# One TensorE product per head and step in the RWKV-7 scan: two kinds of scores and the token-major keys from the same weights

## The chip, the cores and the metric

The kernel runs on one core of a Trainium2 chip. A core has five engines that work through their own instruction streams in order: TensorE (PE; its weight loads are listed apart as PEld), VectorE (DVE), ScalarE (ACT), GpSimd (POOL) and SyncE (SP). SP, ACT and POOL also issue transfers, which 16 DMA engines carry out. The metric is the device time of one execution in microseconds (us); where several executions are compared, their medians are.

## The reference, cut to what matters

The program is a trunk of two layers on 1024 latent tokens and 256 context tokens of width 1024, all in 32-bit floats. The change lies in layer 1, the bidirectional RWKV-7 time mixing. It has 16 heads of width 64. For each head and each of two directions a 64x64 state runs over the context and then over the latent tokens:

```python
def step(S, inp):
    w_t, k_t, v_t, kk_t, kka_t = inp[:5]
    S = (S * w_t[:, :, None, :]
         - jnp.einsum('bhij,bhj->bhi', S, kk_t)[..., None] * kka_t[:, :, None, :]
         + v_t[..., None] * k_t[:, :, None, :])
    y = jnp.einsum('bhij,bhj->bhi', S, inp[5]) if emit else None
    return S, y
```

Here `kk` is the normalised key that is removed, `kka` is that key times a gate, `k` the key that is written, `v` the value, `r` the receptance that reads the state out. Only latent tokens are read out (`emit`).

## The kernel before, in words

The scan is done in chunks of 64 tokens. There are 20 chunks in each direction: steps 0 to 3 are the context, 4 to 19 the latent tokens. Inside a chunk the recurrence becomes matrix products over the 64 tokens; between chunks only the state `SS` is carried. 16 heads are kept as 8 pairs: the first head of a pair (e = 0) in partitions 0 to 63, the second (e = 1) in 64 to 127.

For each step s and direction d an earlier stage has written four feature arrays, which `load` (L1566) brings to one of four buffers `FT` of 128 partitions x 8 pairs x 4 arrays x 64 tokens. The arrays are: 0, the receptance r with its decay; 1, the removed key with its decay; 2 and 3, the two scaled keys (kka and k, divided by the decay). Context chunks have no array 0.

From these, one step early (for n = s + 1), three things are made:

- `scores_k` (L1596): for each head the 64x64 product of array 3 with array 1, into the PSUM tile `sa`. DVE multiplies it with a mask and puts it into partitions 64 to 127 of `Z`. `stack` (L1591) has ACT copy array 1 into partitions 0 to 63 of `Z`.
- `scores_r` (L1608), latent steps only: arrays 2 and 3 together as weights (128 columns) times array 0, into two PSUM tiles `sr`; DVE masks them into `Q`.
- `token_major` (L1626): PE transposes arrays 2 and 3 (4 pairs at a time, tile `tm`), ACT copies them to `TM`, so that the tokens lie along the partitions.

These PSUM tiles turn in a ring of four banks (`scps`). Then come the parts that hang on the state, each with 16 products (each counted twice in the trace, as every 32-bit product is two passes), in another ring of four banks (`chps`):

- `chain_x` (L1664): `Z` times `D`, where `D` holds the carried state in its lower half and the values in its upper half; ACT copies it to `XS`.
- `chain_u` (L1672): the inverse of a triangular matrix (`TT`) times `XS`; ACT writes the negated result into `D` (L1679).
- `readout_state` (L1681) and `readout_values` (L1693), latent steps only: array 0 times the state, and `Q` times `D`, into one tile `yp`; ACT copies it, SP stores it.
- `chain_s` (L1709): `TM` times `D`; DVE adds the old state (L1722) and scales by the decay (L1726).
- `carry` (L1731): in the following iteration, ACT copies the new state into the next `D` (L1736).

`compose1` and `compose2` put the triangular inverses together from blocks of 32 (products of 32x32, tile `p`), once per step, in the iteration of direction 1. `background` supplies work for DVE that `fill` strews between the parts: inversions of the blocks (`scan_invert`, L1511 and L1515) until about step 13, then readout work of the first tokens. `fill` takes on average 1.5, then 2.45, later 1 items.

The loop over steps and directions is under a manual schedule: every engine's instructions stand in the order in which the code emits them. For one iteration (s, d) it is:

```python
load_values(n, d); chain_x(s, d); carry()
scores_k(n, d); token_major(n, d, 0); fill()
chain_u(s, d); [compose1(n)]; token_major(n, d, 4); stack(n, d); fill()
readout_state(s, d); chain_s(s, d); readout_values(s, d); fill()
scores_r(n, d); [compose2(n)]; load(s + 2, d); fill()
```

The two in brackets are there for d = 1 only. After the loop, `readout_weight` reuses the buffers of `Z`, `Q` and `TM` for split weights.

Of the kernel before, what the change touches and what calls it, by code (L numbers as in the profile page):

```python
# [19 lines left out]
D = 1024  # L20
# [19 lines left out]
CH = 64  # L40
# [18 lines left out]
class Trunk:  # L59
# [1466 lines left out]
    def l1_scan(self):  # L1526
        nc, a = self.nc, self.a
        with ExitStack() as es:
# [5 lines left out]
            scps = self.pool(es, "scps1", 4, PSUM)  # L1534
# [3 lines left out]
            FTs = [cp.tile([128, 8, 4, CH], F32, name=f"FT{i}") for i in range(4)]  # L1538
# [4 lines left out]
            st = (slice(0, 64), slice(64, 128))  # L1543

# [9 lines left out]
            W = {s: dict(lat=s >= NCC, F=[0, 0], Z=[0, 0], Q=[0, 0], TM=[0, 0], D=[0, 0], Y=[0, 0]) for s in range(NSTEP)}  # L1554
# [6 lines left out]
            def load(s, d):  # L1561

                w = W[s]
                F = w["F"][d] = FTs[(2 * s + d) % 4]
                f0 = 0 if w["lat"] else 1
                (nc.scalar if s == 0 else nc.gpsimd).dma_start(out=F[:, :, f0:], in_=self.ft[s, d, :, :, f0:])  # L1566
# [24 lines left out]
            def stack(s, d):  # L1591

                for e in range(2):
                    nc.scalar.copy(out=W[s]["Z"][d][0:64, :, e], in_=W[s]["F"][d][st[e], :, 1])

            def scores_k(s, d):  # L1596
                F = W[s]["F"][d]
                Z = W[s]["Z"][d] = zp.tile([128, 8, 2, CH], F32, tag="Z", name="Z")
                sa = scps.tile([128, 8, CH], F32, tag="sc", name="sa")
                for h in range(8):  # L1600
                    for e in range(2):
                        nc.tensor.matmul(out=sa[st[e], h], lhsT=F[st[e], h, 3], rhs=F[st[e], h, 1], start=True, stop=True)  # L1602
                for e in range(2):
                    nc.vector.tensor_tensor(
                        out=Z[64:128, :, e], in0=sa[st[e]], in1=masks[st[e], d, 2:3].to_broadcast([64, 8, CH]), op=ALU.mult
                    )

            def scores_r(s, d):  # L1608

                w = W[s]  # L1610
                if not w["lat"]:
                    return
                F = w["F"][d]
                Q = w["Q"][d] = zp.tile([128, 8, 2, CH], F32, tag="Q", name="Q")
                sr = [scps.tile([128, 8, CH], F32, tag="sc", name="sr") for _ in range(2)]
                for h in range(8):
                    for e in range(2):
                        nc.tensor.matmul(  # L1618
                            out=sr[e][:, h], lhsT=F[st[e], h, 2:4].rearrange("p a t -> p (a t)"), rhs=F[st[e], h, 0], start=True, stop=True
# [598 lines left out]
```

## Time and profile before

| | |
|---|---|
| time before, median of 3 runs | 3549.33 us (3537.39 to 3551.44) |
| profiled execution, its own time | 3559.48 us |
| its span, first to last instruction | 3557.6 us |
| PE busy | 3327.8 us (94%), 26794 instructions |
| PE weight load busy | 2790.3 us (78%) |
| DVE busy | 2054.7 us (58%) |
| ACT busy | 1432.3 us (40%) |
| POOL busy | 342.3 us (10%) |
| mean granted TensorE clock | 0.962 |

The scan's first state product starts at 2212.8 us and its last step ends near 2682 us. Busy shares of the whole span are means over very different stages, so the table is no guide to the scan; stages have to be looked at one by one. A line such as "L1604 DVE TENSOR_TENSOR Z<-sa,masks 64x512" reads: line of the kernel, engine, operation, written tile, read tiles, shape of the output. "Idle before" is the time for which the engine stood idle just ahead of these instructions, with what ended it. "issue" is time in which an engine waited for nothing that the profile shows.

### The profile page before, as it was taken

What the parts mean: (1) busy time and instruction counts of PE and PEld (TensorE: products, weight loads), DVE (VectorE), ACT (ScalarE), POOL (GpSimd) and SP (SyncE); (2) the same over time, 40 slices, a digit from 0 to 9 for tenths busy, and PEclk for the clock granted to TensorE, in tenths of its full rate; (3) what the DMA queues carried; (4) which work ended last, traced back from release to release, by engine and by line L of the source; (5) the groups of instructions that cost most, each with busy time, mean ns of one, the idle gap of its engine ahead of it and who ended that gap; (6) DMA issues with size and microseconds to landing.
All of it is one profiled execution on the core that took longest, in us unless ns stands there. A gap on an engine that the chain in (4) does not pass through costs nothing. (4 is left out here: it accounts for less than half of the span.)

```text
span 3557.6 us, 64666 instructions
## 1 busy us (share of the span) xinstructions
PE 3327.8 (94%) x26794; PEld 2790.3 (78%) x26794; DVE 2054.7 (58%) x3879; ACT 1432.3 (40%) x2667; POOL 342.3 (10%) x450
## 2 busy tenths in 40 slices
PE   8999889999999999989988876899988899999998
PEld 4787767888888888868878776788886788888887
DVE  4255555344444444596658996888775734444446
ACT  4244446312121211266767664655554521111112
POOL 0010110000000000024420001010031200000000
PEclk9999989999999999999989897899988999999999
DMA  8433344222222211143227678777773411111112
GB/s 274 151 92 87 97 131 130 89 83 83 83 84 83 74 46 36 42 148 99 71 69 221 210 233 241 170 185 201 200 204 104 164 50 48 48 48 48 48 48 77
DMA packets 426517, 409.24 MB, mean 115 GB/s; under 512 B 149664, under 2 KB 360480, under 8 KB 422128
## 3 DMA queue, kind: packets, MB, share of 16 engines
q1 hardware_dynamic: 405376, 321.55, 30.8%
q0 software_dynamic: 18624, 81.80, 6.8%
q8 instruction: 210, 3.44, 0.4%
q10 hardware_dynamic: 2224, 1.77, 0.2%
q14 instruction: 83, 0.68, 0.1%
HBM read 292.54 MB, written 112.49 MB: 114 GB/s over the span
## 5 line engine op out<-in xcount | busy, mean ns | idle before, releaser
L916 DVE TENSOR_TENSOR yacc<-yps,yacc 128x512 f32<-128x512 f32 x540 | 369.7, 690 | 305.2 <-PE yps L93 304.8
L74 ACT CAST wh<-st 128x1024 fp32r<-128x1024 f32 x160 | 165.0, 1049 | 759.8 <-PE yps L93 557.8
L93 PE MATMUL yps<-wh,xh 128*128 128x512 f32 x1152 | 453.8, 394 | 5.0 <-DVE yacc L916 3.4
L93 PE MATMUL yps<-wh,xl 128*128 128x512 f32 x1152 | 449.0, 390 | 0.7 <-DVE xl L75 0.7
L93 PE MATMUL yps<-wl,xh 128*128 128x512 f32 x1152 | 449.4, 390 | 0.0
L75 DVE TENSOR_TENSOR wl<-st,wh 128x1024 fp32r<-128x1024 f32 x160 | 194.2, 1228 | 277.4 <-ACT wh L74 277.2
L93 PE MATMUL acc<-h2h,wh 128*128 128x426 f32 (+3 forms) x768 | 275.1, 358 | 3.0 <-ACT y L671 3.0
L93 PEld LDWEIGHTS yps<-wh,xh 128*128 128x128 f32 x1152 | 216.4, 188 | 73.0 <-DVE yacc L916 14.0
L93 PE MATMUL acc<-h2h,wl 128*128 128x426 f32 (+3 forms) x768 | 273.6, 356 | 0.0
L93 PE MATMUL acc<-h2l,wh 128*128 128x426 f32 (+3 forms) x768 | 273.4, 356 | 0.0
L93 PEld LDWEIGHTS yps<-wh,xl 128*128 128x128 f32 x1152 | 216.5, 188 | 47.9 <-DVE xl L75 2.3
L93 PEld LDWEIGHTS yps<-wl,xh 128*128 128x128 f32 x1152 | 216.7, 188 | 44.9 <-issue 1.7
L898 DVE TENSOR_TENSOR r<-r 128x428 f32<-128x428 f32 (+4 forms) x164 | 102.4, 624 | 241.9 <-ACT r L897 241.9
L93 PE MATMUL acc<-mh,wh 128*128 128x256 f32 (+1 forms) x640 | 214.8, 337 | 4.3 <-ACT mh L74 4.2
L93 PE MATMUL acc<-ml,wh 128*128 128x256 f32 (+1 forms) x640 | 214.0, 334 | 0.0
L93 PE MATMUL acc<-mh,wl 128*128 128x256 f32 (+1 forms) x640 | 213.4, 334 | 0.0
L93 PE MATMUL acc<-h2bh,wh 128*128 128x512 f32 (+3 forms) x544 | 211.3, 388 | 1.4 <-ACT wh L74 0.7
L93 PE MATMUL acc<-h2bl,wh 128*128 128x512 f32 (+3 forms) x544 | 211.1, 388 | 1.0 <-DVE h2bl L288 1.0
L93 PE MATMUL acc<-h2bh,wl 128*128 128x512 f32 (+3 forms) x544 | 210.9, 388 | 0.3 <-DVE wl L75 0.3
L897 ACT ACTIVATE r<-acc 128x428 f32<-128x428 f32 (+4 forms) x164 | 89.1, 543 | 293.0 <-PE acc L93 267.9
L93 PEld LDWEIGHTS acc<-h2h,wh 128*128 128x128 f32 x768 | 144.6, 188 | 15.9 <-issue 5.1
L74 ACT CAST xh<-r 128x428 fp32r<-128x428 f32 (+4 forms) x164 | 93.2, 569 | 148.1 <-DVE r L898 148.1
(319 smaller groups left out, 7042.1 us busy)
## 6 DMA issues: line engine op xcount, KB each, us to landing
st<-in_mlp_w SPq DMA_DIRECT2D x128, 512.0 KB
ft<-F SPq DMA_DIRECT2D x64, 512.0 KB
FT<-ft POOLq DMA_DIRECT2D x32, 1024.0 KB, 7.1
adas<-in_ada_w POOLq DMA_DIRECT2D x112, 256.0 KB, 3.8
adas<-in_ada_w SPq DMA_DIRECT2D x80, 256.0 KB
x<-x SPq DMA_DIRECT2D x28, 512.0 KB
bias<-in_bias SPq DMA_DIRECT2D x64, 192.0 KB
ls<-ls SPq DMA_DIRECT2D x80, 128.0 KB
```

The costliest lines, as they stand in the source:

```text
L74: self.nc.scalar.copy(out=hi, in_=src)
L75: self.nc.vector.tensor_tensor(out=lo, in0=src, in1=hi.bitcast(F32), op=ALU.subtract)
L93: self.nc.tensor.matmul(out=ps, lhsT=lhs[x], rhs=rhs[y], start=first and i == 0, stop=last and i == 2)
L897: nc.scalar.activation(out=r, in_=ps, func=AF.Relu)
L898: nc.vector.tensor_tensor(out=r, in0=r, in1=r, op=ALU.mult)
L916: nc.vector.tensor_tensor(out=yacc[t][:, n], in0=ps, in1=yacc[t][:, n], op=ALU.add)
```

## The change

- The buffers `FT` get a fifth slot in front, filled once with the identity by eight DVE copies. The arrays move up by one: 1 is r, 2 the removed key, 3 and 4 the scaled keys. `load` writes slots 1 (or 2) to 4.
- `scores_k`, `scores_r` and `token_major` become one function `scores(s, d, g)` for two pairs, g from 0 to 3. For each head one product has slots 3 and 4 as weights (128 columns) and slots 0, 1, 2 as moving data (192 columns): identity, r and removed key. So it gives the transposed scaled keys, the scores of r and the scores of the removed key. In context steps the r slot is left out, in the last step the identity (128 columns each).
- The result of a group goes into a tile of two PSUM banks, one for each e; there are two such tiles in place of four of one bank.
- `Z` and `Q` become one tile `ZQ`. DVE masks both kinds of scores of a group with one operation; for r's half this is as before, for the other half it also writes partitions 0 to 63, which `stack` then overwrites with the removed key. ACT copies a group's transposed keys to `TM`: four copies in place of two.
- `stack` moves from its place behind `token_major(n, d, 4)` to the end of `carry`, in the following iteration.
- `p1` is written over the block `G` in place of a tile of its own, the state's sum into `SS` itself in place of `t`; the readout's weights 3, 4, 6 and 7 each take one `ZQ` buffer.

```diff
-            scps = self.pool(es, "scps1", 4, PSUM)
+            scps = self.pool(es, "scps1", 2, PSUM)
...
-            FTs = [cp.tile([128, 8, 4, CH], F32, name=f"FT{i}") for i in range(4)]
+            FTs = [cp.tile([128, 8, 5, CH], F32, name=f"FT{i}") for i in range(4)]
...
+            for t in FTs:
+                for e in range(2):
+                    nc.vector.tensor_copy(out=t[st[e], :, 0], in_=self.ident[st[e], st[e]].unsqueeze(1).to_broadcast([64, 8, CH]))
...
-                (nc.scalar if s == 0 else nc.gpsimd).dma_start(out=F[:, :, f0:], in_=self.ft[s, d, :, :, f0:])
+                (nc.scalar if s == 0 else nc.gpsimd).dma_start(out=F[:, :, 1 + f0:], in_=self.ft[s, d, :, :, f0:])
...
-                    nc.scalar.copy(out=W[s]["Z"][d][0:64, :, e], in_=W[s]["F"][d][st[e], :, 1])
...
+                    nc.scalar.copy(out=W[s]["ZQ"][d][0:64, :, e, 1], in_=W[s]["F"][d][st[e], :, 2])
+
+            def scores(s, d, g):
+
+
                 w = W[s]
...
                 F = w["F"][d]
...
+                more = s + 1 < NSTEP
+                if g == 0:
+                    w["ZQ"][d] = zp.tile([128, 8, 2, 2, CH], F32, tag="ZQ", name="ZQ")
+                    if more:
+                        w["TM"][d] = zp.tile([128, 8, 128], F32, tag="TM", name="TM")
+                ps = scps.tile([128, 2, 512], F32, tag="sc", name="sc")
+                p4 = ps[:, :, 0:384].rearrange("p e (j f t) -> p j e f t", j=2, f=3)
+                f = slice(0, 3) if w["lat"] and more else slice(1, 3) if w["lat"] else slice(0, 3, 2)
+                for j in range(2):
                     for e in range(2):
                         nc.tensor.matmul(
...
+                            out=p4[:, j, e, f], lhsT=F[st[e], 2 * g + j, 3:5].rearrange("p a t -> p (a t)"), rhs=F[st[e], 2 * g + j, f],
+                            start=True, stop=True,
                         )
...
+                hs = slice(2 * g, 2 * g + 2)
+                if w["lat"]:
                     nc.vector.tensor_tensor(
...
+                        out=w["ZQ"][d][:, hs].rearrange("p j e f t -> p j e (f t)"),
+                        in0=ps[:, :, 0:384].rearrange("p e (j n) -> p j e n", j=2)[:, :, :, CH:],
+                        in1=masks[:, d, 1:3].rearrange("p f t -> p (f t)").unsqueeze(1).unsqueeze(1).to_broadcast([128, 2, 2, 2 * CH]),
+                        op=ALU.mult,
                     )
...
+                else:
+                    nc.vector.tensor_tensor(
+                        out=w["ZQ"][d][64:128, hs, :, 1], in0=p4[64:128, :, :, 2],
+                        in1=masks[64:128, d, 2:3].unsqueeze(1).to_broadcast([64, 2, 2, CH]), op=ALU.mult,
                     )
...
+                if more:
+                    nc.scalar.copy(out=w["TM"][d][:, hs].rearrange("p j (e i) -> p j e i", e=2), in_=p4[:, :, :, 0])
...
-                w["p1"] = zs.tile([128, 2, 8, 32], F32, tag="p1s", name="p1s", bufs=1)
+                w["p1"] = w["G"]
...
+                    nc.vector.tensor_tensor(out=SS[d], in0=sp, in1=SS[d], op=ALU.add)
+                    src = SS[d]
...
+                    stack(s, d)
...
-                    scores_k(n, d)
-                    if n + 1 < NSTEP:
-                        token_major(n, d, 0)
+                    for g in range(2):
+                        scores(n, d, g)
                     fill()
                     chain_u(s, d)
                     if d:
                         compose1(n)
-                    if n + 1 < NSTEP:
-                        token_major(n, d, 4)
-                    stack(n, d)
+                    scores(n, d, 2)
                     fill()
                     readout_state(s, d)
                     chain_s(s, d)
                     readout_values(s, d)
                     fill()
-                    scores_r(n, d)
+                    scores(n, d, 3)
                     if d:
                         compose2(n)
```

More of the change, by code (lines that the diff above doesn't have):

```diff
@@ L1552, in rows_of @@
                 return t[c * CH:(c + 1) * CH]
-            W = {s: dict(lat=s >= NCC, F=[0, 0], Z=[0, 0], Q=[0, 0], TM=[0, 0], D=[0, 0], Y=[0, 0]) for s in range(NSTEP)}
+            W = {s: dict(lat=s >= NCC, F=[0, 0], ZQ=[0, 0], TM=[0, 0], D=[0, 0], Y=[0, 0]) for s in range(NSTEP)}
             lt_, ltt_ = self.lt_, self.ltt_
@@ L1593, in stack @@
                 for e in range(2):
[L1594 to L1606, printed above, removed]
@@ L1668, in chain_x @@
                     for e in range(2):
-                        nc.tensor.matmul(out=xp[st[e], h], lhsT=w["Z"][d][:, h, e], rhs=w["D"][d][:, h, e], start=True, stop=True)
+                        nc.tensor.matmul(out=xp[st[e], h], lhsT=w["ZQ"][d][:, h, e, 1], rhs=w["D"][d][:, h, e], start=True, stop=True)
                 nc.scalar.copy(out=XSs[d], in_=xp)
@@ L1688, in readout_state @@
                         nc.tensor.matmul(
-                            out=yp[st[e], h], lhsT=w["F"][d][st[e], h, 0], rhs=SS[d][st[e], h], start=h == 0, stop=True,
+                            out=yp[st[e], h], lhsT=w["F"][d][st[e], h, 1], rhs=SS[d][st[e], h], start=h == 0, stop=True,
                             skip_group_check=True,
@@ L1700, in readout_values @@
                         nc.tensor.matmul(
-                            out=yp[st[e], h], lhsT=w["Q"][d][:, h, e], rhs=w["D"][d][:, h, e], start=False, stop=True, skip_group_check=True
+                            out=yp[st[e], h], lhsT=w["ZQ"][d][:, h, e, 0], rhs=w["D"][d][:, h, e], start=False, stop=True, skip_group_check=True
                         )
@@ L1781, in l1_scan @@
             for d in range(2):
-                scores_k(0, d)
+                for g in range(4):
+                    scores(0, d, g)
                 stack(0, d)
-                for h0 in (0, 4):
-                    token_major(0, d, h0)
                 load(1, d)
@@ L1886, in readout_weight @@
         ip, zp = self.rwp
-        pool, tag = {
-            8: (ip, "M"), 0: (ip, "X"), 1: (zp, "TM"), 2: (ip, "BK"), 3: (zp, "Z"), 4: (zp, "Q"), 5: (zp, "TM"), 6: (zp, "Z"), 7: (zp, "Q"),
-        }[k]
-        w = [pool.tile([128, D], F32R, tag=tag, name=f"rwo{i}{k}") for i in "hl"]
+        if k in (3, 4, 6, 7):
+            w = zp.tile([128, 2, D], F32R, tag="ZQ", name=f"rwo{k}")
+            w = [w[:, i] for i in range(2)]
+        else:
+            pool, tag = {8: (ip, "M"), 0: (ip, "X"), 1: (zp, "TM"), 2: (ip, "BK"), 5: (zp, "TM")}[k]
+            w = [pool.tile([128, D], F32R, tag=tag, name=f"rwo{i}{k}") for i in "hl"]
         self.split(w[0], w[1], self.rst.pop(k))
```

21 lines of the change are left out of this document (removed).

## The prediction

> **What bounds the kernel now.** The change touches only the scan, so I read the table of stages first. Columns: stretch, length, then busy time of PE, PE weight load, DVE, ACT, POOL (instructions in brackets), granted clock, DMA share, GB/s.
>
> ```profile
> span 3557.6 us, 64666 instructions
> ```
>
> ```profile
> 2212.80:2288.70 75.90, 64.97 (x1668) 57.78 (x1666) 57.42 (x136) 50.44 (x86) 7.61 (x12) 0.91 0.81 174
> 2288.70:2538.20 249.50, 228.81 (x5926) 209.98 (x5922) 216.65 (x521) 141.57 (x240) 23.67 (x41) 0.93 0.68 183
> 2538.20:2667.80 129.60, 114.88 (x2947) 105.59 (x2944) 84.06 (x100) 77.31 (x129) 35.75 (x23) 0.92 0.76 218
> ```
>
> These are steps 0 to 3 (mainly context), 4 to 13 (block inversions run between the steps on DVE) and 14 to 18 (early readout runs between them). PE looks like the bound of all three. The chain of waits in order of time (start, length, work) shows one iteration of one direction, 2394.20 to 2403.64, and what follows the other:
>
> ```profile
> 2388.28 1.90 PE sp L1716 x32
> ...
> 2394.20 1.08 PE xp L1669 x32
> 2395.29 1.08 PE sa L1602 x32
> 2396.36 0.59 PE tm L1632 x4
> 2396.95 1.08 PE up L1677 x32
> 2398.03 0.59 PE tm L1632 x4
> 2398.61 1.08 PE yp L1688 x32
> 2399.69 1.08 PE sp L1716 x32
> 2400.78 0.93 PE yp L1700 x32
> 2401.71 1.93 PE sr L1618 x32
> ...
> 2414.48 1.13 PE p L1658 x64
> 2415.61 1.08 PE xp L1669 x32
> 2416.69 1.08 PE sa L1602 x32
> ```
>
> PE has no gap there: 9.44 us for direction 0 and 11.97 (to 2415.61) for direction 1, which also builds the inverses. But the second view, DVE's groups in steps 4 to 13 (busy, mean | idle before them), says that DVE is no less full:
>
> ```profile
> L1515 DVE TENSOR_TENSOR X<-X,tmp 128x112 f32<-128x112 f32 (+15 forms) x196 | 66.8, 341 | 6.7
> L1511 DVE TENSOR_TENSOR tmp<-X,M 128x112 f32<-128x112 f32 (+15 forms) x196 | 66.4, 339 | 5.1
> L1604 DVE TENSOR_TENSOR Z<-sa,masks 64x512 f32<-64x512 f32 x40 | 27.6, 690 | 9.7 <-PE sa L1602 8.9
> L1622 DVE TENSOR_TENSOR Q<-sr,masks 128x512 f32<-128x512 f32 x40 | 25.6, 682 | 0.1
> L1722 DVE TENSOR_TENSOR t<-sp,SS 128x512 f32<-128x512 f32 x21 | 14.5, 692 | 8.9 <-PE sp L1716 8.4
> ```
>
> Of DVE's idle 249.50 - 216.65 = 32.9 us only 8.9 + 8.4 = 17.3 are waits for PE. The other 15.6 are gaps of some 0.03 us between instructions (6.7 us over 196 in the first row). If DVE never waited, the stage would take 249.5 - 17.3 = 232.2 us, 11.6 per iteration: more than the 10.7 that PE needs on average for 9.44 and 11.97. DVE and PE are bounds together, and PE's stalls are what keeps DVE waiting.
>
> **The change, part by part: PE.** An iteration loses sa, two tm and sr: 1.08 + 0.59 + 0.59 + 1.93 = 4.19 us. It gains 16 products of 64 rows by 128 weight columns with 192 moving columns. Two heads of a pair sit in different row halves and run together, and each product is two passes, so that is 16 pair-passes. Layer 0 has the same form with 256 and 384 columns:
>
> ```profile
> 314.12 0.70 PE L731 MATMUL sc<-kT,qT 64*128 64x256 f32 x4
> 314.66 0.81 PE L736 MATMUL sl<-kT,qT 64*128 64x384 f32 x4
> ```
>
> ```profile
> L736 PE MATMUL sl<-kT,qT x128: 482/482/844, 160.8 to 459.4; 64*128 64x384 f32 x128
> ```
>
> Four sl records last 0.81 us in all and the last one 0.482, so the second pair-pass starts 0.33 us after the first with 384 columns; sr gives 1.93/16 = 0.12 with 64 columns. If streaming covers the weight load, 192 columns cost half of sl's: 0.16, or 2.6 us for 16. If load and stream add up, the line through 0.12 and 0.33 gives 0.20, or 3.2 us. The sc row decides: from 314.12 to 314.66 lie one load and two pair-passes of 256 columns. The line's 0.245 for each would leave 0.05 us for the load; the proportion's 0.22 leaves 0.10, close to sr's 0.12, which with so few columns is nearly all load. I take 2.6, a saving of 1.6 us (other end 1.0). Context steps use 128 columns: between 0.12 and 0.16 per pair-pass, some 1.9 us against 1.08 + 1.18; the last step 1.9 against 1.08 + 1.93. PE's work shrinks by 30 x 1.6 + 2 x 1.1 + 8 x 0.35 = 53 us at most, the whole prize.
>
> The Trainium skill, "TensorE: Matmul & The Clock Gate", Part 3, on what overlaps, speaks against it: a weight load overlaps a running product only in another row group, and here each pair fills both. By that rule the 3.2 us or more would hold. It is counted below as a mechanism.
>
> **DVE.** Two key masks (2 x 0.690) and two score masks (2 x 0.682) become four operations of 128x512 from PSUM, 4 x 0.69: 2.76 for 2.74, nothing saved. The operand shapes are new; 2.6 to 3.2 bounds them. The addition that now writes in place costs the same. So the 232.2 us stand, and steps 4 to 13 can gain from 0 to 17.3 us. With 1.6 us more slack per iteration PE catches up part of a stall (20.7 us idle in the stage, and a granted clock of 0.93). Against it stand two score buffers (of two banks each) instead of four, which tie PE to DVE's last two mask operations. I take half: -9.
>
> **ACT.** Its queue in the same iteration, and the nearest row for the smaller copy:
>
> ```profile
> 2395.44 0.58 ACT L1670 COPY XS<-xp 128x512 f32<-128x512 f32 x1
> 2396.05 1.26 ACT L1736 COPY D<-SS 64x512 f32<-64x512 f32 x2
> 2397.21 0.57 ACT L1635 COPY TM<-tm 128x512 f32<-128x512 f32 x1
> 2398.14 1.21 ACT L1679 ACTIVATE D<-up 64x512 f32<-64x512 f32 x2 [0.35 <-PE up L1677]
> 2399.37 0.58 ACT L1635 COPY TM<-tm 128x512 f32<-128x512 f32 x1
> 2399.98 1.25 ACT L1594 COPY Z<-FT 64x512 f32<-64x512 f32 x2
> ```
>
> ```profile
> L1251 ACT COPY vt<-acc 128x256 f32<-128x256 f32 x40 | 15.2, 380 | 1.3 <-PE acc L93 1.0 <-issue 0.4
> ```
>
> Two copies of 128x512 (1.15) become four of 128x256 (4 x 0.38 = 1.52). The two key copies (1.25) move from behind the negated copy (L1679) to right behind the carried states, and there they wait for DVE's fourth mask. In front of the negated copy then stand XS 0.58, D 1.26, keys 1.25 and two copies of 0.76, so it starts 3.85 us after xp's end (2.85 above: 2398.14 against 2395.29) and ends at 5.1. What is queued behind it: the second sp, and readout values. From xp's end PE has two groups of products (1.3 us), up (1.08), then the third group, which needs the first group's copy: 0.58 + 1.26 + 1.25 + 0.38 = 3.5. PE stands idle from 2.4 to 3.5 in direction 0; in direction 1 the 1.13 us of inverse products fill it. Third group 0.65, yp 1.08: sp is reached at 5.2, just past the copy's 5.1. So ACT takes back 1.1 of the 1.6 us in direction 0 and nothing in direction 1: 1.05 saved on average.
>
> In steps 14 to 18 DVE has room (84.06 of 129.60) and this sum applies: 10 iterations x 1.05 = 10.5 us, but readout work also stands in DVE's and ACT's queues ahead of masks and copies. I take -5 (bounds -16, all of PE's 1.6, and +3).
>
> In steps 0 to 2 there is no readout product to cover the negated copy; PE already waits for it:
>
> ```profile
> 2239.18 1.09 PE L1716 MATMUL sp<-D,TM 128*64 128x64 f32 x29 [0.29 <-ACT D L1679]
> ```
>
> Six iterations with the copy 1.25 + 0.76 - 0.57 = 1.44 later are +8.6 us at most, 0 at least where a stall is longer; +4.
>
> **DMA, and the start.** The buffer has five slots, so a load lands in runs of 1 KB instead of one of 8 KB per partition. The context loads (runs of 768 bytes) are the nearest rows:
>
> ```profile
> FT<-ft POOLq DMA_DIRECT2D x32, 1024.0 KB, 7.1
> ...
> FT<-ft POOLq DMA_DIRECT2D x6, 768.0 KB, 9.3
> ```
>
> ```profile
> 2400.23 0.53 POOL L1566 DMA_DIRECT2D FT<-ft  x1 [9.70 <-ACT TM L1635]
> ```
>
> By bytes the context rate would give 12.4 us, so 7.1 to 12.4. The load issued at 2400.23 is first read at 2416.69, 16.5 us later: hidden, with 4 us to spare at the worse end. The Trainium skill, "DMA: Bandwidth & Descriptors", Specifications, puts full rate at 512 bytes and more, which would leave 7.1. If the cover were gone, the 5 us would fall on each of 32 iterations.
>
> Eight copies of the identity (64x512, at most 8 x 0.69 = 5.5 us) come onto DVE at the scan's start, among the last feature units. An idle stretch there nearly holds them:
>
> ```profile
> 2191.88 0.42 DVE L1388 TENSOR_TENSOR ks<-kd 128x256 f32<-128x256 f32 x1 [5.12 <-PE bp L1413]
> ```
>
> I count +1.5 (0 to +8, should the larger buffers or the copies delay the first loads). Fewer tiles (p1s, t), the merged buffers and the readout weights in them cost nothing: their old readers are done an iteration earlier.
>
> **Sum.** -9 - 5 + 4 + 1.5 = -8.5 us. The profiled execution took 3559.48 us (span and 1.9 around it), 10 above the median; the difference is carried over: 3549.33 - 8.5 = 3541. Own range 3527 to 3553.
>
> **Rivals.** *PE's gain arrives whole.* DVE's 17.3 us of waiting vanish and steps 14 to 18 save 10 x 1.6: -33, or 3516. For it: DVE's waits are all for PE. Against: ACT's order in direction 0.
>
> *ACT becomes the bound* (the other side). The key copies wait behind DVE's fourth mask and stand in front of the negated copy. It decides as soon as that mask ends over 1.8 us (0.58 + 1.26) past xp's end and DVE is not the slower anyway. In 16 iterations (0 to 2, 14 to 18) then +1.44 each and no PE gain: +23, or 3572. For it: readout operations between the masks. Against: ACT is busy 77.31 of 129.60 us.
>
> *The products are dearer.* Load and stream add up, 3.2 us for 4.19; ACT's 1.1 leaves nothing, steps 0 to 3 and the start keep +5.5: 3555. The sl and sc rows speak against it. The same result if loads come late now and then.
>
> The clock acts in all cases: sp took 1.90 us at 2388.28 and 1.08 at 2399.69. More idle PE may lower it; where DVE is the bound this costs nothing.
>
> **Chances.** Forecast 0.52, whole gain 0.20, ACT bound 0.13, dearer products 0.15. A measurement here can tell some 0.5%, 17.7 us: below 3531.6 is faster, above 3567.1 slower. Faster: 0.13 of the forecast and 0.19 of the whole gain, 0.32. Slower: 0.11 of ACT and 0.02 of dearer products, 0.13. Same: 0.55. The range reaches from the whole gain to half of ACT's loss: 3514 to 3562.
>
> **What would show it.** Right: the new products take 2.5 to 2.7 us per iteration; PE's busy time in the scan falls by some 45 us while DVE's stays near 217 in steps 4 to 13 and its waits for PE fall below 10; PE waits in front of the third group for ACT or DVE. Wrong: PE idle no longer than before (whole gain), sp waiting for the negated copy in steps 4 to 18 (ACT), pair-passes of 0.2 us, waits on FT loads, or a first xp over 5 us later.

## The result and the profile after

The changed kernel takes 3561.55 us (median of 11 runs, 3557.53 to 3578.39), the kernel before 3547.84 us (11 runs, 3537.39 to 3554.24). The ratio is 1.0051, 95% interval 1.0034 to 1.0067: slower by some half a per cent (13.7 us between the two medians), where a small gain of 8.5 us was forecast. A second set of runs gave 3567.11 us and 1.0047 (1.0034 to 1.0061).

The first profiled execution of the kernel before lay 10 us above its median. The comparison of stages below therefore uses a second one, whose own time was 3548.8 us. The view is the table of stages again (stretch, length, busy time of PE, weight load, DVE, ACT, POOL, granted clock, DMA share, GB/s), for steps 0 to 3, 4 to 13 and 14 to 18. First the kernel before, second execution:

```profile
2210.60:2285.90 75.30, 66.63 (x1668) 59.26 (x1666) 57.53 (x136) 50.43 (x86) 7.60 (x12) 0.88 0.75 176
2285.90:2534.50 248.60, 223.87 (x5924) 205.47 (x5920) 216.15 (x520) 141.35 (x240) 23.69 (x41) 0.96 0.68 184
2534.50:2659.80 125.30, 114.84 (x2950) 105.83 (x2944) 82.80 (x100) 77.20 (x129) 35.33 (x23) 0.92 0.76 223
```

Then the changed kernel, whose profiled execution took 3557.53 us:

```profile
2206.60:2297.00 90.40, 71.88 (x1537) 62.64 (x1536) 64.64 (x163) 49.97 (x99) 9.48 (x12) 0.85 0.73 160
2297.00:2541.10 244.10, 205.32 (x5126) 177.98 (x5120) 204.99 (x507) 141.66 (x280) 30.75 (x42) 0.97 0.71 181
2541.10:2668.90 127.80, 102.90 (x2567) 90.55 (x2560) 81.53 (x99) 77.88 (x146) 38.19 (x23) 0.95 0.78 219
```

PE's busy time falls, from 405.3 to 380.1 us over the three rows. The stages don't follow: 15.1 us are lost in steps 0 to 3, 4.5 won in steps 4 to 13, 2.5 lost in 14 to 18. The scan also begins 4.0 us earlier, which is within the scatter of its start (between 2204 and 2213 us over all the profiles of this case). That makes 9 of the 13.7 us; the other 5 lie between this execution, the fastest of the 11, and the median, and no profile here shows them.

Where PE stands still is plain in the groups of the changed kernel (busy, mean ns | idle before them). The first row is of steps 0 to 3, the second of steps 4 to 13:

```profile
L1614 PE MATMUL sc<-FT 64*128 64x128 f32 (+1 forms) x256 | 28.9, 355 | 14.6 <-ACT TM L1632 11.7 <-issue 3.0
...
L1614 PE MATMUL sc<-FT 64*128 64x192 f32 x640 | 73.0, 351 | 25.6 <-ACT TM L1632 25.5
```

PE stands idle in front of the new products for 14.6 us in steps 0 to 3 (11.7 of them wait for ACT) and 25.6 in steps 4 to 13. Of the 15.1 us that steps 0 to 3 lose, 9.8 are more idle time of PE (18.5 us against 8.7); the other 5.3 are its own busy time (71.88 against 66.63), at a granted clock of 0.85 against 0.88. What ends the wait is ACT's copy of an earlier group to `TM`, which frees a PSUM tile. And that copy waits too. The waits of steps 4 to 13 in the changed kernel (total us, times, longest):

```profile
ACT TM L1632 <- DVE ZQ L1620: 58.3, 30, 4.1
...
PE sc L1614 <- ACT TM L1632: 25.5, 31, 1.7
DVE ZQ L1620 <- PE sc L1614: 17.8, 16, 2.9
...
DVE SS L1718 <- PE sp L1713: 10.1, 9, 1.9
```

ACT's copy waits for DVE's mask of the same PSUM tile, though the copy reads other columns than the mask and nothing that the mask writes. No step of the prediction has a copy wait for the mask of its own tile. DVE's waits for PE, 17.3 us before, are now 27.9.

ACT's queue in an iteration of direction 0 shows at which copy it stands (timeline, idle before in brackets):

```profile
2393.03 0.37 ACT L1632 COPY TM<-sc 128x256 f32<-128x256 f32 x1 [3.01 <-DVE ZQ L1620]
...
2394.49 0.59 ACT L1667 COPY XS<-xp 128x512 f32<-128x512 f32 x1
2395.10 1.26 ACT L1732 COPY D<-SS 64x512 f32<-64x512 f32 x2
2396.38 1.25 ACT L1597 COPY ZQ<-FT 64x512 f32<-64x512 f32 x2
2397.53 0.63 ACT L1632 COPY TM<-sc 128x256 f32<-128x256 f32 x2
2398.06 1.21 ACT L1676 ACTIVATE D<-up 64x512 f32<-64x512 f32 x2
2399.64 0.37 ACT L1632 COPY TM<-sc 128x256 f32<-128x256 f32 x1 [0.37 <-DVE ZQ L1620]
...
2405.80 0.37 ACT L1632 COPY TM<-sc 128x256 f32<-128x256 f32 x1 [3.20 <-DVE ZQ L1620]
2406.07 0.59 ACT L1667 COPY XS<-xp 128x512 f32<-128x512 f32 x1
```

Groups 0 and 1 are copied at 2397.53, group 2 at 2399.64, group 3 at 2405.80. Added up over these rows of all 20 iterations, ACT stands 51.3 us ahead of the copy of group 3, 5.3 ahead of that of group 2 and 0.3 ahead of the other two. The chain of waits says why (start, length, work):

```profile
2397.63 0.28 ACT TM L1632
...
2397.95 0.94 PE sc L1614 x8
...
2401.22 0.69 DVE SS L1718
...
2401.94 0.69 DVE SS L1722
2402.64 0.34 DVE tmp L1511
...
2404.76 0.40 DVE X L1515
2405.16 0.61 DVE ZQ L1620
...
2405.80 0.37 ACT TM L1632
2406.17 0.49 ACT XS L1667
```

Group 3's products were done at 2402.8, but in DVE's queue a fill (three pairs of inversion operations, 2402.64 to 2405.16) stood ahead of its mask. So the mask was late, ACT's copy waited for it, and `XS`, the two carried states and the two key copies stood behind that copy. `xp` was ready at 2403.9; `XS` was copied at 2406.1. The first two rows are the same link at the head of the iteration: group 2's products start as group 0's copy ends.

### The profile page after: what moved, and what is told of

Read it like the earlier page. It is cut to its first block, busy times and chain, and to the rows that moved or that the text cites. A ratio compares the mean times of both kernels' runs of the same rounds, so it can differ in the third digit from the quotient of the medians.

```text
span 3555.8 us, 62116 instructions
## 1 busy us (share of the span) xinstructions
PE 3298.3 (93%) x25466; PEld 2747.9 (77%) x25466; DVE 2050.4 (58%) x3903; ACT 1435.6 (40%) x2743; POOL 353.7 (10%) x450
## 5 line engine op out<-in xcount | busy, mean ns | idle before, releaser
L93 PEld LDWEIGHTS yps<-wh,xh 128*128 128x128 f32 x1152 | 216.2, 188 | 70.7 <-DVE yacc L916 11.7
L1614 PE MATMUL sc<-FT 64*128 64x192 f32 (+1 forms) x1280 | 146.0, 356 | 64.0 <-ACT TM L1632 50.7
L1614 PEld LDWEIGHTS sc<-FT 64*128 64x128 f32 x1280 | 106.1, 205 | 80.3 <-ACT TM L1632 60.8
```

Source lines behind the costliest of these rows:

```text
L93: self.nc.tensor.matmul(out=ps, lhsT=lhs[x], rhs=rhs[y], start=first and i == 0, stop=last and i == 2)
L1614: nc.tensor.matmul(out=p4[:, j, e, f], lhsT=F[st[e], 2 * g + j, 3:5].rearrange("p a t -> p (a t)"), rhs=F[st[e], 2 * g + j, f], start=True ...
```

## The experiments

All times are medians; ratios are against the kernel before, run beside it on the same chip (its medians lay between 3543.9 and 3547.1 us). Stages are lengths in us of steps 0 to 3, 4 to 13 and 14 to 18 in the profiled execution; the last column is how long ACT stood ahead of the copies of groups 0, 1, 2, 3 in steps 4 to 13, added up over ACT's timeline.

| kernel | median | ratio (95%) | 0-3 | 4-13 | 14-18 | ACT ahead of copies 0, 1, 2, 3 |
|---|---|---|---|---|---|---|
| before_again | 3548.80 (one run) | | 75.3 | 248.6 | 125.3 | |
| after_again | 3567.11 | 1.0047 (1.0034 to 1.0061) | 89.2 | 240.7 | 132.3 | 0.0, 0.3, 4.2, 52.0 |
| stack_late | 3553.88 | 1.0019 (1.0010 to 1.0028) | 84.0 | 248.2 | 129.3 | 4.8, 3.2, 1.5, 53.5 |
| stack_before | 3549.85 | 1.0011 (1.0000 to 1.0021) | 81.8 | 241.4 | 124.1 | |
| copy_first | 3564.56 | 1.0040 (1.0027 to 1.0054) | 83.1 | 247.4 | 131.6 | |
| loop_cut | 3576.76 | 1.0077 (1.0064 to 1.0091) | 89.6 | 254.8 | 129.0 | |
| noinv_before | 3547.10 | 1.0008 (0.9993 to 1.0023) | 76.2 | 245.2 | 122.2 | |
| noinv_after | 3542.50 | 0.9998 (0.9983 to 1.0013) | 79.3 | 238.4 | 127.3 | |
| respaced | 3543.80 | 0.9994 (0.9982 to 1.0006) | 81.0 | 244.8 | 118.8 | 4.9, 3.3, 1.7, 49.0 |
| one_fill | 3548.69 | 1.0015 (0.9998 to 1.0031) | 86.3 | 238.3 | 127.4 | 9.1, 3.5, 9.1, 27.7 |
| fills_only | 3544.04 | 0.9989 (0.9975 to 1.0004) | 84.4 | 234.6 | 121.1 | 9.2, 2.9, 36.2, 20.3 |
| late_copy | 3557.01 | 1.0037 (1.0023 to 1.0051) | 89.0 | 243.9 | 133.0 | 1.1, 1.4, 7.8, 9.3 |
| two_runs | 3560.16 | 1.0043 (1.0027 to 1.0059) | 87.0 | 243.4 | 133.5 | 50.2, 5.8, 1.3, 2.4 |
| two_runs_f | 3534.95 | 0.9965 (0.9954 to 0.9977) | 86.2 | 231.2 | 120.4 | 35.5, 5.4, 18.2, 4.6 |
| two_runs_c | 3557.94 | 1.0030 (1.0019 to 1.0040) | 87.7 | 236.0 | 129.7 | |
| two_runs_3f | 3543.23 | 0.9985 (0.9972 to 0.9997) | 77.8 | 241.9 | 128.6 | 13.4, 5.2, 51.2, 5.7 |
| two_runs_stack | 3537.08 | 0.9972 (0.9960 to 0.9984) | 81.4 | 235.0 | 126.8 | 15.0, 3.3, 40.5, 5.3 |
| two_runs_ctx | 3533.11 | 0.9962 (0.9948 to 0.9977) | 81.4 | 232.4 | 122.8 | 37.2, 5.6, 18.9, 3.9 |

A stage of one profiled execution can stand some us off another of the same kernel (244.1 and 240.7, 127.8 and 132.3 for the changed kernel), so single stages are read only where they differ by more, or where two pairs agree.

**The two kernels again,** unaltered:

> The kernel before once more, for a second profile: the first profiled execution was slower than any of its other times, and four profiles of changed kernels have their first scan product at 2205 to 2213 us where that profile has it at 2213. Expected by all theories: the same stage table for the scan within 5 us a stage (steps 0 to 3: 76, 4 to 13: 250, 14 to 18: 130), and a first scan product between 2205 and 2213 us.

> The changed kernel once more, unaltered, for a second profile and a second set of times. Theory 'loop': in every iteration one loop sets the pace: DVE's mask of the last group, the copies of ACT behind it (keys to TM, XS, carried state, removed keys, keys to TM), the third group's products on PE, DVE's mask, fill and state update, and back to the last mask. It expects the ratio to before again near 1.005, ACT's wait for DVE's mask in front of the TM copies again near 58 us in steps 4 to 13, and steps 0 to 3 again 10 to 15 us longer than before. Rival 'chance': the profile pair shows the changed kernel 2 us shorter while the medians show it 14 us longer, so the difference could sit in stalls of the load queues that fall by chance; it expects a ratio between 0.998 and 1.002 and a stage table in which another stage carries the difference.

Measured: 3548.8 and 3567.11 us. Steps 0 to 3 again carry the loss (75.3 and 89.2 us), this time with 7.0 us in steps 14 to 18 beside it, and ACT's wait for masks in steps 4 to 13 is again 57.9 us, as the loop theory expected.

**The moved key copies**, first put back behind the negated copy in the changed kernel:

```diff
 def carry():                       # per carried state
-    stack(s, d)
+    stacks.append((s, d))
...
 chain_u(s, d)
+stack_all()
```

> Only the copy of the removed keys moves, from the carried states to behind the negated copy (and so out of the way of the copies that the third group waits for). Theory 'loop': 1.25 us leave the loop in each of 38 iterations; DVE's work catches part of it, so 10 to 25 us faster than the changed kernel, a ratio to before of 0.998 to 1.002; PE's wait for the TM copy in front of the products falls from 50 us to below 30. Rival 'DVE': DVE's full queue sets the pace in steps 4 to 13 whatever ACT does; only steps 0 to 2 gain, some 5 us, ratio 1.003 to 1.004.

It measured 3553.88 us, 13 less than the changed kernel beside it, within what was expected. PE's wait for the copies, over the whole scan, fell from 50.0 to 30.9 us, just short of the 30 that were named. Then the reverse, the move alone in the kernel before:

```diff
 def carry():
+    stack(s, d)
...
-stack(n, d)
 fill()
```

> The kernel before, with one part of the change alone: stack (two ACT copies) moved to the end of carry, so it stands in front of ACT's negated copy. Theory (the moved stack costs time where no readout product covers the negated copy, steps 0 to 2, whatever the new products do): steps 0 to 3 get 4 to 7 us longer than the kernel before (75 to 80-82 us), steps 4 to 13 change by less than 3 us, time +4 to +8 us (3551 to 3555, ratio 1.001 to 1.0025). Rival (the stack hurts only together with the new score groups, since there it must wait for their fourth mask): no stage changes by over 2 us, time 3545 to 3549.

```profile
2206.70:2288.50 81.80, 69.76 (x1667) 62.23 (x1666) 61.30 (x146) 48.90 (x84) 7.62 (x12) 0.85 0.75 172
2288.50:2529.90 241.40, 224.73 (x5924) 205.88 (x5924) 214.02 (x513) 139.55 (x240) 24.75 (x43) 0.96 0.70 186
```

The stage rows of this kernel: steps 0 to 3 take 6.5 us longer than before, as expected, and the time rises by 4.4. So the move by itself costs about what the prediction gave it (+4), in the steps where no readout product covers the negated copy; the interval of the ratio, 1.0000 to 1.0021, begins at no change at all. That steps 4 to 13 came out 7 us shorter was not expected; putting the copies back in the changed kernel made them 4 to 7.5 longer. Two pairs agree, yet the cause is open.

**Which reader comes first.** The wait joins two readers of one PSUM tile. Here ACT's copy is emitted ahead of DVE's mask:

```diff
+if more: nc.scalar.copy(out=w["TM"]...)
 nc.vector.tensor_tensor(out=w["ZQ"]...)
-if more: nc.scalar.copy(out=w["TM"]...)
```

> Only the order of the two readers of a group's PSUM tile is turned round: ACT copies the keys first, DVE masks afterwards. Theory 'loop': the TM copy of the last group, XS and the carried states no longer stand behind DVE's last mask, which takes some 2 us out of the loop, but the removed keys still wait for that mask; 5 to 20 us faster than the changed kernel, ratio 0.999 to 1.004, and ACT's wait for DVE's masks in front of the TM copies is gone. Rival 'DVE': DVE now waits for ACT in front of each mask instead, and DVE is the fuller engine: no gain or a loss, ratio 1.005 to 1.010.

The waits of this kernel in steps 4 to 13:

```profile
PE sc L1614 <- DVE ZQ L1622: 30.8, 24, 3.2
DVE ZQ L1622 <- ACT TM L1620: 26.7, 21, 3.8
```

The wait is turned round: now DVE waits for ACT, and PE for DVE. So the second reader waits for the first, whichever comes first in the code. The time stays: 1.0040 is the very end of the first expectation's range, and below the rival's. With the carried states behind groups 0 and 1, and the key copies late, in addition:

```diff
+for g in range(2): scores(n, d, g)
 carry()
-for g in range(2): scores(n, d, g)
```

> Both orders at once, and the copies of the carried state go behind the first two groups' TM copies: ACT's queue is XS, two TM copies, carried state, negated copy, removed keys. Theory 'loop': ACT and DVE are cut apart, PE waits for the third group hardly at all, and the forecast's DVE bound is what remains: 15 to 35 us faster than before, ratio 0.990 to 0.996. Rival 'DVE': steps 4 to 13 stay within 5 us of the 249.5 us of before, ratio 0.997 to 1.001.

This was the slowest of all, 3576.76 us, where both expectations had it at 1.001 or less: DVE's waits for ACT grew to 37.5 us and PE's for DVE to 32.4. A kernel in which the two readers are independent was not tried: they would need PSUM tiles of their own.

**Whether DVE is the bound.** Both kernels with the arithmetic of the later block inversions left out, which takes some 128 us off DVE in steps 4 to 13:

```diff
+if b < 2:
     nc.vector.tensor_tensor(out=tmp, ...)
     nc.vector.tensor_tensor(out=X[...], ...)
```

> The kernel before without the arithmetic of the block inversions of steps 4 to 19 (their multiplications and subtractions on DVE are left out; the transfers stay), so DVE has room in the scan. PE's work of 10.7 us per iteration is then the bound; steps 4 to 13 go from 249.5 to some 235 us.

> The changed kernel with the same inversions left out. Theory 'loop' (DVE's fill between the masks is what makes the loop long): without the fill the masks follow the products at once, and PE's smaller work shows: steps 4 to 13 some 10 to 20 us shorter than in the kernel before without inversions, the time 10 to 25 us shorter. Rival 'ACT and ring': the order of ACT's copies and the two score buffers alone cost the gain; the two kernels without inversions are within 5 us, or the changed one is slower.

Steps 4 to 13, the kernel before without inversions, then the changed one:

```profile
2285.50:2530.70 245.20, 224.50 (x5927) 205.90 (x5922) 88.19 (x128) 141.46 (x240) 23.15 (x43) 0.96 0.70 185
```

```profile
2287.00:2525.40 238.40, 206.10 (x5126) 182.61 (x5120) 88.81 (x128) 143.17 (x280) 29.30 (x42) 0.95 0.75 189
```

With DVE at 88 of 245 us, the kernel before takes the time that it always took (1.0008), and steps 4 to 13 stay at 245.2 us instead of falling to the 235 that were expected. So DVE was not a bound in it. PE was, busy for 224.5 of 245.2 us; of the other 20.7, 16.6 are "issue" and 4.1 waits for a load. In the second profile of the kernel before itself, too, PE's waits in steps 4 to 13 do not name DVE:

```profile
PE tm L1632 <- ACT TM L1635: 3.0, 1, 3.0
```

The changed kernel loses nothing once DVE's queue is short (0.9998), and steps 4 to 13 are shorter: the loss comes from what stands in DVE's queue. But it gains little. It is 4.6 us below the kernel before without inversions, and 6.8 shorter in steps 4 to 13, where 10 to 25 and 10 to 20 were expected; within 5 us was the rival's figure. So the missing gain is not explained by the fills alone.

**The fills.** A fill is what stands there. First, with the key copies late, two fills behind group 2 and none ahead of group 3:

```diff
 scores(n, d, 2)
 fill()
+fill()
 readout_state(s, d)
 chain_s(s, d)
 readout_values(s, d)
-fill()
 scores(n, d, 3)
```

> The changed kernel with the removed keys copied behind the negated copy, and with the fill that stood between the state update and the last mask moved up to behind the third mask, so that DVE's last mask follows the state update at once and ACT's TM copy and XS behind it do not wait for a fill. Theory 'loop': 15 to 30 us faster than the changed kernel, ratio to before 0.994 to 0.999; ACT's wait for masks in front of the TM copies falls from 58 us in steps 4 to 13 to below 35. Rival 'DVE': the masks of the first groups are late instead; ratio 1.001 to 1.004, as with the removed keys moved alone (1.0019).

3543.8 us, and by the ratios (0.9994 and 1.0019) some 9 us less than `stack_late`, which has the fills at the old places. Yet ACT's wait, expected to fall from 58 us to below 35, did not: 49.0 us are left ahead of group 3's copy alone. Two fills still stand in DVE's queue between the masks of groups 2 and 3, as before. What the 9 us are is open. Then the changed kernel with nothing but fills moved, two behind groups 0 and 1 and two at the end:

> The changed kernel with nothing but fills moved: two behind groups 0 and 1, two at the end of the iteration, none behind group 2 or the values' readout. Loop theory: from one state sum to the next, through DVE's queue and back over PE, stand two fills of 1.7 us, the masks of groups 3 and 0 (0.69 each), group 0's copy 0.37, group 2 0.85, state readout 1.08, state product 1.08 and the two state operations 1.38: 9.5 us, the same as in the changed kernel (there the second of the two fills stands between the masks). So the time stays within 5 us of the changed kernel, 3556 to 3567, ratio 1.003 to 1.006. Rival (what counts is that fills are spread evenly over the masks, two and two, as in two_runs_f): 3535 to 3550, ratio below 1.0015.

Waits of this kernel in steps 4 to 13:

```profile
ACT TM L1632 <- DVE ZQ L1620: 69.9, 64, 3.5
...
PE sc L1614 <- ACT TM L1632: 22.0, 18, 2.2
DVE SS L1718 <- PE sp L1713: 7.0, 8, 1.5
DVE ZQ L1620 <- PE sc L1614: 6.1, 13, 2.4
```

The loop that I had summed (9.5 us, unchanged) called for 3556 to 3567; it took 3544.04, within the rival's range, so that theory falls. How long ACT waits does not decide, for it waits longer than before (69.9 against 58.3 us). What changed with the time is where: the wait is spread over groups 2 and 3, DVE's own waits for PE drop from 27.9 to 13.1 us, and the loss is gone. Then only the one fill that the chain shows:

```diff
-fill()
 scores(n, d, 3)
+fill()
```

> The changed kernel with one fill moved, from in front of group 3 to right behind it. Theory (this fill of about 1.7 us delays group 3's mask, its copy waits for it, and the next XS, the carried states and the stack stand behind that copy): ACT's wait at group 3's copy falls from 51 us to under 35 in steps 4 to 13, steps 0 to 3 to 86 us or less, time 3543 to 3552, ratio 0.9985 to 1.0015. Rival (it was the other fills that fills_only moved): 3556 to 3567, ratio 1.003 to 1.006.

3548.69 us, about two thirds of the loss recovered by one line, and ACT's wait ahead of group 3's copy falls from 51.3 to 27.7 us, as expected. Lastly the copy itself moved behind `XS`, with the fills left alone:

```diff
-if more: nc.scalar.copy(out=w["TM"]...)     # for g == 3
...
 nc.scalar.copy(out=XSs[d], in_=xp)
+while copies: copies.pop()()
```

> The changed kernel with group 3's ACT copy emitted behind the next XS copy instead of in front of it; nothing else moved. If the price of the wait is that XS (and so the chain of the other direction) stands behind it: 3545 to 3554, and PE's waits in front of the second product (up) for XS fall. Rival (the copy's wait is paid through group 1, which needs the slot that the copy frees, and through the carried states behind it, wherever XS stands): 3557 to 3568, ratio 1.003 to 1.006.

```profile
PE sc L1616 <- ACT TM L1636: 20.2, 24, 2.7
ACT TM L1636 <- DVE ZQ L1622: 19.3, 32, 2.5
DVE ZQ L1622 <- PE sc L1616: 17.5, 17, 3.5
```

The wait at that copy is nearly gone (9.3 us), and PE no longer waits for `XS` ahead of `up` (4.0 us in the changed kernel), yet little is won (3557.01, at the lower edge of the rival's range): PE waits for the copies for 20.2 us where it waited 25.5. So the price isn't that `XS` stands behind the copy. A likely reading, not tested by itself, is that group 1 of the next iteration, which needs the PSUM tile that this copy frees, has to wait for DVE's mask either way.

**Two runs of products in place of three.** On top of late key copies, groups 2 and 3 stand together behind the state's readout; the kernels differ in where the fills are, and `two_runs_c` also has the copy ahead of the mask:

```diff
 for g in range(2): scores(n, d, g)
-fill()
+fill()              # two_runs, two_runs_c: 1, two_runs_f: 2, two_runs_3f: 3
 chain_u(s, d); stack_all(); [compose1(n)]
-scores(n, d, 2)
-fill()
 readout_state(s, d)
+for g in range(2, 4): scores(n, d, g)
 chain_s(s, d)
+fill()              # not in two_runs_3f
 readout_values(s, d)
-fill()
-scores(n, d, 3)
+fill()              # two_runs, two_runs_c only
```

> The changed kernel with the four score groups in two runs of two (0 and 1 behind chain_x as now, 2 and 3 between readout_state and chain_s), and stack behind the negated copy; as many fills. Theory (a start of a run of products costs PE some 0.2 us, and the two-slot ring stalls PE where mask and copy of a group come within 2 us of the next one): the products take 3.0 us per iteration in place of 3.2, groups 2 and 3 cover the negated copy for the second state product, and the distance from one pair of groups to the next is 2.2 us and 3.1 us; steps 0 to 3 at 80 us or less, PE's waits for ACT's TM copy below half (under 13 us in steps 4 to 13), time 3532 to 3543, ratio 0.996 to 0.999. Rival (what binds is the number of masks and copies that stand between a pair of groups, 1.4 us of DVE and 0.75 of ACT one behind the other, so a pair is the worst form): PE waits as long as in the changed kernel, 3546 to 3556.

> As two_runs, but the fill that stood behind readout_values stands behind the first pair of groups: two fills between the masks of groups 1 and 2 instead of one. Theory (background items in DVE's queue ahead of a mask stall PE through the ring): longer waits of PE for TM copies in front of groups 2 and 3, 3 to 8 us slower than two_runs. Rival (the place of fills does not matter once a pair of groups has two slots free): within 2 us of two_runs.

> As two_runs, with each group's ACT copy emitted ahead of DVE's mask, so that the mask waits for the copy. Theory (the order of the two readers only says which engine's queue the other waits for; ACT's queue is the emptier one between the pairs): within 4 us of two_runs, ACT's waits for masks gone and DVE's waits for ACT over 15 us in steps 4 to 13. Rival (the mask behind the copy puts ACT's XS copy and carried state in front of DVE's work): 8 us or more slower than two_runs.

Both first expectations failed, in opposite directions: 3560.16 for the one, 3534.95 for the other, 25 us apart by the place of a fill, where no more than 8 was expected. With one fill between the two pairs and three up to the next pair, ACT stands 50.2 us ahead of group 0's copy; with two and two it is 35.5 and 18.2 (groups 0 and 2), and PE's wait falls too. The rows of `two_runs` and then of `two_runs_f`, steps 4 to 13:

```profile
PE sc L1614 <- ACT TM L1632: 16.1, 12, 2.7
```

```profile
PE sc L1614 <- ACT TM L1632: 9.4, 9, 2.1
```

```profile
2294.50:2537.90 243.40, 209.06 (x5128) 190.14 (x5122) 209.41 (x509) 145.87 (x280) 30.76 (x41) 0.92 0.73 183
2297.70:2528.90 231.20, 201.59 (x5126) 182.86 (x5122) 207.87 (x508) 145.24 (x281) 30.76 (x41) 0.96 0.77 198
```

These rows show that the waits are not the whole of it. Over steps 0 to 18 the stages of `two_runs` are 26.1 us longer, and 16.5 of these are PE's own busy time (387.26 against 370.73 us for the same products), at a granted clock of 0.76, 0.92 and 0.86 in the three stages against 0.81, 0.96 and 0.94. This is no accident of one execution: over whole executions the granted clock was 0.956 to 0.959 in all runs of `two_runs`, 0.953 to 0.960 in those of `two_runs_c` and 0.959 to 0.965 in those of `two_runs_f`. Why this order is granted less clock is not known. PE also waits for the loads of `FT` in both, 12.4 and 8.9 us.

The copy ahead of the mask (`two_runs_c`, 3557.94) is no better than the mask first, as expected; both have the fills one and three, and the low clock. DVE's waits for ACT are 12.2 us, where over 15 were expected. A third fill moved the same way, to see whether more is better:

> As two_runs_f, with one more fill moved from behind the state product to behind groups 0 and 1 (three there, one at the end). Loop theory: sums of the loop are 10.1 us in two_runs (3560), 8.4 in two_runs_f (3535), 6.7 here, against an iteration of 11.6; once the loop is well below the iteration no more is to be had, so within 6 us of two_runs_f and not slower by more than 3: 3529 to 3538. Rival (evenness decides): as bad as two_runs, 3550 or more.

3543.23: neither of the two expectations. The wait has gone over to the copy of group 2 (51.2 us). So of the three places two and two is the best, and something is lost on either side of it. The last two put the order of `respaced` into steps 0 to 2 of `two_runs_f`, or its key copies from step 3 on back behind the carried states:

```diff
+if s > 2: stack_all()             # two_runs_stack, behind carry()
...
+if s < 3: ...                     # two_runs_ctx: groups and fills as in respaced
+else: ...                         # as in two_runs_f
```

> As two_runs_f, but in steps 0 to 2 the order of respaced (groups 2 and 3 apart, two fills behind group 2). If respaced's 81.0 us in steps 0 to 3 comes from this order, steps 0 to 3 fall from 86.2 to 80-82 and the time by 4 to 6 us to 3529 to 3531. Rival (the context's loss is PE's dearer products and the clock, whatever the order): 85 us or more, time within 2 us of two_runs_f.

> As two_runs_f, but from step 3 on stack stands behind the carried states as in the changed kernel. stack_late and stack_before suggest that this place costs 6 us in steps 0 to 3 and gains 4 to 7 in steps 4 to 13. If so here too: steps 4 to 13 fall from 231.2 to 225-228, time 3528 to 3532. Rival (DVE binds these steps in two_runs_f, 232.2 being the sum without its waits, so a free ACT is worth nothing, and the copies in front of the negated copy hold up the second state product): 231 to 236, time 3534 to 3541.

`two_runs_ctx`:

```profile
2205.80:2287.20 81.40, 67.42 (x1540) 59.09 (x1538) 64.67 (x161) 50.51 (x100) 8.70 (x12) 0.88 0.83 180
2287.20:2519.60 232.40, 200.44 (x5126) 182.26 (x5122) 206.69 (x507) 144.66 (x280) 30.83 (x41) 0.96 0.77 195
2519.60:2642.40 122.80, 99.67 (x2564) 90.99 (x2564) 80.61 (x101) 78.94 (x145) 38.58 (x23) 0.94 0.77 217
```

Steps 0 to 3 take 81.4 us, as expected, and the time is 3533.11 us, 2 us above the range that was expected and within 2 us of `two_runs_f` (3534.95), as the rival had it. That the order of `respaced` brings the 81.4 us is not shown: `two_runs_stack`, which is the same as `two_runs_f` in steps 0 to 2, has 81.4 us as well, where `two_runs_f` had 86.2. This is the best of the versions: 0.9962, interval 0.9948 to 0.9977, some 14 us below the kernel before, but not told apart from `two_runs_f`. The early key copies gain nothing in the later steps (235.0 us; 3537.08), as the rival expected.

## Why the prediction was wrong

**The step that failed first is in the part on ACT.** It put the new copies into ACT's queue behind ACT's own work only, and had them wait for nothing but their products. In the program the two readers of a PSUM tile take turns, so a copy also waits for the mask, and through it for every fill that DVE has ahead of that mask. This is the 58.3 us of ACT and the 25.5 us of PE in steps 4 to 13, and 11.7 us of PE in steps 0 to 3. The prediction named the mask of the fourth group, but had only the key copies wait for it; the two score buffers that "tie PE to DVE's last two mask operations" were given no price of their own. With one fill moved the ratio falls from 1.0047 to 1.0015, with all moved it is 0.9989. The prediction's own sign of being right, DVE's waits for PE below 10 us in steps 4 to 13, failed at 27.9.

**"DVE and PE are bounds together" was wrong.** With DVE's work cut by 128 us the kernel before is no faster. DVE's waits for PE (17.3 us) were a consequence of PE's being the bound, and 232.2 us no floor set by DVE in that kernel. The upper end of the "0 to 17.3 us" for steps 4 to 13 was reached by another order of the work (248.6 to 231.2 in `two_runs_f`), with DVE still waiting 9.7 us for PE; of the 9 that were forecast the changed kernel got 4.5. In `two_runs_f` DVE is the fuller engine (207.87 us against PE's 201.59 of 231.20). Whether it is the bound there was not tested.

**The new products: the mechanism right, the term mis-sized.** The timeline of PE in the changed kernel:

```profile
2393.55 1.57 PE L1614 MATMUL sc<-FT 64*128 64x192 f32 x16
2395.12 1.15 PE L1674 MATMUL up<-XS,TT 64*64 64x64 f32 x32
...
2401.89 0.92 PE L1614 MATMUL sc<-FT 64*128 64x192 f32 x8
2402.74 1.15 PE L1666 MATMUL xp<-D,ZQ 128*64 128x64 f32 x32
```

And two groups in `two_runs_f`:

```profile
2384.20 1.57 PE L1614 MATMUL sc<-FT 64*128 64x192 f32 x16
2385.70 1.43 PE L1713 MATMUL sp<-D,TM 128*64 128x64 f32 x32
```

A group alone takes 0.85 us up to the next product (2401.89 to 2402.74), two together 1.50 (2384.20 to 2385.70; in the 1.57 of the first rows `up` also waits for `XS`, which is copied until 2395.08). The four pair-passes between cost (1.50 - 0.85)/4 = 0.16 each, as predicted, so streaming does cover the weight load. The Trainium skill, "TensorE: Matmul & The Clock Gate", Part 3, has a weight load overlap a running product only in another row group. By that rule load and stream would add up here, since each pair fills both row groups; the trace has the pass at 0.16 and decides against it. But each run of products pays some 0.2 us once (0.85 - 4 x 0.16). With three runs that is 1.50 + 0.85 + 0.85 = 3.2 us per iteration and not 2.6; the saving is 1.0, the prediction's other end for another reason. PE's busy time in the scan fell by 25 us, where "some 45" was given. In steps 0 to 3 the new products even take more than the old, 28.9 us busy against 26.4 for `sa`, `tm` and `sr` (at granted clocks of 0.85 and 0.88), where a small saving was counted.

**Steps 0 to 2** were given +4 for the moved key copies. The move alone costs 6.5 us in steps 0 to 3 of the kernel before (4.4 in the time); 3.7 of them fall in steps 0 to 2 (53.6 to 57.3 us from first xp to first xp), so this term was about right. The other loss there has two parts, and the runs do not price them apart: PE's wait for copies and masks again (11.7 us), and PE's own busy time, 5.3 us more in place of less. Six of the 15.1 us stay in the best version (81.4 against 75.3), and why is not settled: late key copies, two-run order and `respaced`'s order gave from 77.8 to 87.7 us.

**Steps 14 to 18** were given -5. They came out 2.5 us longer, and 7.0 in the second profile; ACT waits 26.9 us for masks there and PE 12.8 for copies. The prediction did say that readout work stands ahead of masks and copies, and halved its gain for it; no gain was left.

**The clock** was said to act in all cases and got no term. In steps 0 to 3 it was 0.85 and 0.86 in the two executions of the changed kernel, 0.91 and 0.88 in those of the kernel before. Whether the waits bring this, or chance, the runs don't tell.

**The start** was given +1.5. The first xp came 4 us earlier (2206.6 against 2210.6), but the kernel before and its own variants alone scatter between 2206.7 and 2212.8, so this term is neither borne out nor refuted. **The loads** were hidden as predicted, but for one wait of 1.5 us: they land in

```profile
FT<-ft POOLq DMA_DIRECT2D x32, 1024.0 KB, 7.5
```

7.5 us, against 7.1 before, inside the 7.1 to 12.4 given. **The masks** of 128x512 with their new operands take 0.685 us on average (80 of them in steps 4 to 13), as predicted.

**The rivals.** The measured 3561.55 lies between two of them. "ACT becomes the bound" (3572) came nearest in its place, the queue of ACT behind the fourth group's mask; its mechanism, key copies in front of the negated copy, was worth 4.4 us in the kernel before (`stack_before`) and 13 in the changed one (`stack_late`), there together with the wait for the mask. "Products are dearer" (3555) had the right price, 3.2 us, and the wrong cause. "PE's gain arrives whole" was reached by no order of the work: the best came to 14 of its 33 us. The forecast's own range ended at 3553; that the time still falls just inside the outer range, 3514 to 3562, is luck, for that end was reached by half of ACT's loss and not by a copy's wait for a mask.

**What stays open.** By which path the late copy is paid: through the slot that group 1 needs (which `late_copy` suggests) or through DVE's order; no sum of one loop that I made fits all orders. How much of the differences between orders is waits and how much the granted clock. And 5 of the 13.7 us that the profiles do not show.

## What to carry to other kernels

When several engines read the same PSUM tile, write down for each reader which other reader it follows, and what stands ahead of that one in its own queue: a saving on one engine can hang on another engine's background work. Filler placed for an old order has to be placed anew with the new one; here the place of a single fill changed the time by some 11 us in the changed kernel, and by 25 in another order of it, where the whole change was to gain 8.5. To learn whether a busy engine is a bound, take work off it and see whether the time moves; two engines that both look full need not both be bounds.

## What the runs showed of the hardware

- Two readers of one PSUM tile on ACT and DVE ran one behind the other in these programs, in whichever order they were emitted (58.3 us of ACT's waits with the mask first; 26.7 of DVE's with the copy first). Whether the chip or the program's own ordering asks for it is not told by these runs.
- A run of the new score products cost some 0.2 us once (0.85 - 4 x 0.16), on top of 0.16 us per pair-pass.
- A load into runs of 1 KB landed in 7.5 us instead of 7.1, but POOL took longer to issue it, 0.88 us against 0.53:

```profile
2400.49 0.88 POOL L1569 DMA_DIRECT2D FT<-ft  x1 [11.13 <-ACT TM L1632]
```
- The granted clock in steps 4 to 13 did not fall though PE stood idle longer (38.8 us against 20.7 and 24.7): 0.97 in the changed kernel, against 0.93 and 0.96 in the two executions of the kernel before. In steps 0 to 3 it lay between 0.74 (`two_runs_c`) and 0.95 (`respaced`) over all the profiles; what sets it these runs don't tell.
